# A small early store to the output, from a second DMA queue, in a pooling kernel that streams its input

**The chip and the metric.** One core of a Trainium2 chip. The metric is the device time of one execution in microseconds (us). A profile's span is some 1.8 us shorter than the device time of the same execution (92.5 for 94.24). Times in a trace are counted from the span's start. In this document "an engine" without a name is one of the core's 16 DMA engines. A transfer of 128 rows gives each engine 8 of them; in the trace's packet records a row is one packet. A transfer lands when the last engine has told that its rows are done.

## The reference

Average pooling over 2x2x2 windows of a float32 tensor. Cut to what matters:

```python
batch, channels, d, h, w = (8, 32, 32, 32, 32)      # kernel_size = 2
window = x[:, :, 2*i:2*i+2, 2*j:2*j+2, 2*k:2*k+2]
result[:, :, i, j, k] = np.mean(window, axis=(-3, -2, -1))
```

Seen as 256 rows (batch times channel), a row has 32,768 input elements (128 KB) and 4,096 output elements (16 KB). The input is 33.55 MB, the output 4.19 MB.

## The kernel before

The rows are taken in two halves of 128 partitions (t = 0, 1). Each half comes in by column blocks: six loads of 4 MB (rows of 32 KB), then four of 2 MB (rows of 16 KB). VectorE makes three passes over each block. Results collect in one tile for each half, which go out in three stores at the end.

```python
pool_in = ctx.enter_context(tc.tile_pool(name="pin", bufs=5))
pool_out = ctx.enter_context(tc.tile_pool(name="pout", bufs=1))
obuf = [pool_out.tile([P, 16 * KF], F32, name=f"obuf{t}") for t in range(2)]   # KF = 256
# ... cut: plan of loads; pool_unit = two tensor_adds and a tensor_tensor_reduce
for t, k0, parts in plan:
    tin = pool_in.tile([P, 32 * KF], F32, tag="tin", name="tin")
    for kb in parts:                       # shortened
        nc.sync.dma_start(out=v, in_=xv[t * P:(t + 1) * P, ...])
    # ... pool_unit on each part
for t, k0, kb in [(0, 0, 16), (1, 0, 14), (1, 14, 2)]:
    nc.sync.dma_start(
        out=ov[t * P:(t + 1) * P, k0 * KF:(k0 + kb) * KF],
        in_=obuf[t][:, k0 * KF:(k0 + kb) * KF])
```

All loads and stores are issued by the Sync engine (SP) and run in one DMA queue, in the order of issue: ten loads, then the stores of 2 MB, 1.79 MB and 256 KB.

Of the kernel before, what the change touches and what calls it, by code (L numbers as in the profile page):

```python
# [1 line left out]

# [4 lines left out]

F32 = mybir.dt.float32
KF = 256


@with_exitstack
def kernel(
    ctx: ExitStack,
    tc: tile.TileContext,
    x: bass.AP,
    kernel_size: int,
    out: bass.AP,
):
    nc = tc.nc  # L20
    assert kernel_size == 2, "only kernel_size == 2 supported"

    B, C, D, H, W = x.shape
    P = nc.NUM_PARTITIONS
    assert (B * C, D, H, W) == (2 * P, 32, 32, 32)
    add = mybir.AluOpType.add



    xv = x.rearrange("b c d h w -> (b c) (d h w)")  # L30
    ov = out.rearrange("b c d h w -> (b c) (d h w)")




    pool_in = ctx.enter_context(tc.tile_pool(name="pin", bufs=5))
    pool_out = ctx.enter_context(tc.tile_pool(name="pout", bufs=1))
    obuf = [pool_out.tile([P, 16 * KF], F32, name=f"obuf{t}") for t in range(2)]
    dummy = pool_out.tile([P, 1], F32, name="dummy")


    plan = [
        (0, 0, (32,)),
        (0, 32, (32,)),
        (0, 64, (32,)),
        (0, 96, (32,)),
        (1, 0, (32,)),
        (1, 32, (32,)),
        (1, 64, (16, 16)),
        (1, 96, (16, 16)),  # L50
    ]

    def pool_unit(buf, t, k0, kb):

        od = kb // 8
        a = buf.rearrange("p (o dd e) -> p o dd e", o=od, dd=2)
        b = buf[:, :od * 1024]
        nc.vector.tensor_add(  # L58
            out=b.rearrange("p (o e) -> p o e", o=od), in0=a[:, :, 0], in1=a[:, :, 1])
        bv = b.rearrange("p (e ww) -> p e ww", ww=2)  # L60
        c = buf[:, od * 1024:od * 1536]
        nc.vector.tensor_add(out=c, in0=bv[:, :, 0], in1=bv[:, :, 1])  # L62
        cv = c.rearrange("p (j hh k) -> p j hh k", hh=2, k=16)
        o0 = k0 * KF // 8
        nc.vector.tensor_tensor_reduce(  # L65
            out=obuf[t][:, o0:o0 + od * 256].rearrange("p (j k) -> p j k", k=16),
            in0=cv[:, :, 0], in1=cv[:, :, 1],
            scale=0.125, scalar=0.0, op0=add, op1=add, accum_out=dummy[:, :],
        )

    for t, k0, parts in plan:
        tin = pool_in.tile([P, 32 * KF], F32, tag="tin", name="tin")
        views = []
        o = 0
        for kb in parts:
            v = tin[:, o * KF:(o + kb) * KF]
            nc.sync.dma_start(
                out=v, in_=xv[t * P:(t + 1) * P, (k0 + o) * KF:(k0 + o + kb) * KF])
            views.append((v, k0 + o, kb))
            o += kb  # L80
        for v, k, kb in views:
            pool_unit(v, t, k, kb)
# [5 lines that stand above are left out]
            in_=obuf[t][:, k0 * KF:(k0 + kb) * KF],  # L88
        )


# [1 line left out]
_INS = ['x', 'kernel_size']  # L93
_OUTS = [((8, 32, 16, 16, 16), 'float32')]

_NUMBERS = {'kernel_size': 2}


# [26 lines left out]
```

## Time and profile before

| | before |
|---|---|
| device time, first three runs | 94.03 us (93.86 to 94.03) |
| span of the profiled run | 92.5 us |
| packets' time in the one DMA queue | 96.5% of 16 engines' span |
| VectorE busy | 64.0 us, 69% |
| end of VectorE's last pass | 85.95 us |

Read the DMA row first: a queue whose packets take 96.5% of the engines' span leaves the kernel little but to move fewer bytes or to move them in faster packets.

### The profile page before, as it was taken

To read this page: it belongs to the slowest core of one execution; us is meant where nothing else is said; L and a number is where in the kernel's file an instruction comes from. 1 tells how busy PE (TensorE), PEld (TensorE's weight loads), DVE (VectorE), ACT (ScalarE), POOL (GpSimd) and SP (SyncE) were. 2 spreads that over 40 slices of the span, in tenths; PEclk is the share of its full clock that TensorE was granted. 3 is DMA by queue.
4 is the path that set the end of the run, shared out by engine and by line. 5 is a ranking of instruction groups with operands and counts; after the bars stand their busy time and mean duration, and the time that the engine had idled before them with its cause. 6 is when DMAs were issued, how large, how long until landed. Compare 5 with 4: busy or idle time off the path is not lost.

```text
span 92.5 us, 103 instructions
## 1 busy us (share of the span) xinstructions
DVE 64.0 (69%) x40; POOL 0.2 (0%) x4
## 2 busy tenths in 40 slices
DVE  0000049992999299948996699849999999999100
POOL 0000000000000000000000000000000000000000
DMA  7699999998999999999989999989999999999992
GB/s 198 255 454 454 454 454 454 439 397 369 439 439 411 454 454 454 454 454 439 397 383 425 397 454 454 454 369 425 454 418 411 439 432 354 333 447 439 411 406 105
DMA packets 1872, 37.75 MB, mean 408 GB/s; under 512 B 208, under 2 KB 208, under 8 KB 336
## 3 DMA queue, kind: packets, MB, share of 16 engines
q1 hardware_dynamic: 1872, 37.75, 96.5%
HBM read 33.55 MB, written 4.19 MB: 408 GB/s over the span
## 4 chain that ended last, share of the span: by engine, by line
DMA 57%; DVE 35%; issue 0%; DVEq 0%
DMA tin<-in_x_dram 57%; DVE tin L58 19%; DVE tin L62 10%; DVE obuf L65 6%; DVE dummy L65 0%; DVEq L120 0%
## 5 line engine op out<-in xcount | busy, mean ns | idle before, releaser
L58 DVE TENSOR_TENSOR tin<-tin 128x4096 f32<-128x4096 f32 (+1 forms) x10 | 35.7, 3570 | 21.3 <-DMA tin<-in_x_dram 21.3
L62 DVE TENSOR_TENSOR tin<-tin 128x2048 f32<-128x2048 f32 (+1 forms) x10 | 18.6, 1865 | 0.3
L65 DVE CUSTOM_DVE_ANT_1 obuf<-tin 128x1024 f32<-128x1024 f32 (+1 forms) x10 | 10.1, 1011 | 0.3
L65 DVE DVE_READ_ACCUMULATOR2_ANT dummy<- 128x1 f32 x10 | 0.8, 82 | 0.0
L106 POOL MEMSET const-bfloat16-1.0<- 128x1 bf16 x1 | 0.1, 101 | 0.0
L106 POOL MEMSET const-uint8-127<- 128x1 uint8 x1 | 0.1, 101 | 0.0
L106 POOL MEMSET const-float32-0.0<- 128x1 f32 x1 | 0.1, 98 | 0.2 <-issue 0.2
L106 POOL MEMSET const-float32-1.0<- 128x1 f32 x1 | 0.1, 98 | 0.0
## 6 DMA issues: line engine op xcount, KB each, us to landing
tin<-in_x_dram SPq DMA_DIRECT2D x6, 4096.0 KB, 35.2
tin<-in_x_dram SPq DMA_DIRECT2D x4, 2048.0 KB, 38.0
out_dram<-obuf SPq DMA_DIRECT2D x1, 2048.0 KB, 36.6
out_dram<-obuf SPq DMA_DIRECT2D x1, 1792.0 KB, 9.1
out_dram<-obuf SPq DMA_DIRECT2D x1, 256.0 KB, 5.5
```

The lines of the kernel that those rows point to most:

```text
L58: nc.vector.tensor_add(out=b.rearrange("p (o e) -> p o e", o=od), in0=a[:, :, 0], in1=a[:, :, 1])
L62: nc.vector.tensor_add(out=c, in0=bv[:, :, 0], in1=bv[:, :, 1])
L65: nc.vector.tensor_tensor_reduce(out=obuf[t][:, o0:o0 + od * 256].rearrange("p (j k) -> p j k", k=16), in0=cv[:, :, 0], in1=cv[:, :, 1], s ...
L106: nc = _bacc.Bacc("TRN2", target_bir_lowering=False, num_devices=1)
```

## The change

Zeros are written early to the first 128 columns of the first 128 output rows. The likely intent is to have the first write to the output happen while the first load is only starting. The real store writes the same elements again later.

```diff
+    first = pool_out.tile([P, 128], F32, name="first")
+    nc.vector.memset(first[:, :], 0.0)
+    nc.scalar.dma_start(out=ov[0:P, 0:128], in_=first[:, :])
```

## The prediction

> **What bounds the kernel now.** The kernel reads 33.55 MB and writes 4.19 MB on one core, all from one DMA queue (the SP queue). I read the page first, then the two lists of waits (the engines' and the queue's own), then stretches of the span. The page's slices and its DMA part:
>
> ```profile
> DMA  7699999998999999999989999989999999999992
> GB/s 198 255 454 454 454 454 454 439 397 369 439 439 411 454 454 454 454 454 439 397 383 425 397 454 454 454 369 425 454 418 411 439 432 354 333 447 439 411 406 105
> q1 hardware_dynamic: 1872, 37.75, 96.5%
> HBM read 33.55 MB, written 4.19 MB: 408 GB/s over the span
> ```
>
> The DMA engines are busy from the first slice to the last but one; the packets' time is 96.5% of 16 engines' whole span of 92.5 us, that is 89.3 us of every engine. What is missing is 1.7 us in front and 1.4 us behind. A slice whose GB/s is low (the first two, and slices 34 and 35) is still full of busy engines: there packets are slow, not absent. Stretches cut at these places say it better (columns: stretch in us, its length, DVE busy, POOL busy, clock, DMA share, GB/s):
>
> ```profile
> 0.00:1.70 1.70, 0.00 (x0) 0.20 (x4) 1.00 0.00 0
> ...
> 4.10:50.00 45.90, 31.80 (x16) 0.00 (x0) 1.00 1.01 434
> 50.00:77.50 27.50, 23.92 (x17) 0.00 (x0) 1.00 0.98 419
> 77.50:80.00 2.50, 2.47 (x4) 0.00 (x0) 1.00 1.01 301
> 80.00:86.00 6.00, 5.85 (x7) 0.00 (x0) 1.00 1.01 432
> ```
>
> The sustained rate is 432 to 434 GB/s, 27 GB/s an engine. In the single packet records a 32 KB row takes 1.213 us, except the first one of each engine, which takes 1.39 to 2.09 us (mean 1.81): the start costs about 0.6 us an engine. At 77.5 to 80 us the rate falls to 301 GB/s: two 16 KB packets of each engine take about 1 us in place of 0.611. Over the 640 packets of that size the mean is 632.5 ns, so an engine, with 40 of them, loses 40 x 21.5 ns = 0.86 us, nearly all there.
>
> The chain on the page ends in VectorE work, and it is the wrong guide. The queue's own waits and the groups by form:
>
> ```profile
> SPq L86 <- DVE dummy L65: 44.0, 3, 31.3
> ...
> SPq L120 <- DMA out_dram<-obuf: 5.1, 1, 5.1
> ```
>
> ```profile
> L58 DVE TENSOR_TENSOR tin<-tin 128x2048 f32<-128x2048 f32 x4 | 9.1, 2286 | 0.0
> L62 DVE TENSOR_TENSOR tin<-tin 128x1024 f32<-128x1024 f32 x4 | 4.9, 1224 | 0.1
> L65 DVE CUSTOM_DVE_ANT_1 obuf<-tin 128x512 f32<-128x512 f32 x4 | 2.8, 692 | 0.1
> ```
>
> VectorE is through at 85.95 us; then the program waits 5.1 us for stores. The last store (256 KB) is issued at 85.98 us, but the 1.79 MB store in front of it, issued at 81.8 us, keeps the engines busy until 90.6 us. So VectorE is some 4.6 us early and the engines' queue sets the end: what adds time to an engine's packets adds it to the total, and what takes it away takes it from the total. The last 2 MB unit of VectorE (2.29 + 1.22 + 0.69 = 4.2 us) fits into that slack.
>
> **What the Trainium skill says.** "DMA: Bandwidth & Descriptors", section "Issuing engines are not separate DMA queues": DMAs of all issuers run on the same 16 engines and interleave; a second issuer saves only issue time. Nothing is to be saved here: the SP queue issues the first five loads from 0.73 to 3.14 us, and their data last until 51 us. That the second queue shares the engines, no trace of before shows, since it has one queue. The same page, "Queues, rings and completion order": an engine goes round its queues packet by packet. So the small store will not wait for the 20 MB of loads queued before it; it slips in between rows of the first load. Not visible before either. "Perfetto Trace Analysis", section "DMA Instruction — HWDGE (DVE, Sync)": the DMA instruction's span is only lock wait and descriptor generation, and the generator is used by one issuer at a time. The trace agrees as to the first: an issue takes 0.33 to 0.53 us, its data land 5.5 to 49 us later.
>
> **The change, part by part.** It removes nothing. It adds one tile of 128x128 zeros, a VectorE memset, one 64 KB store from the ScalarE queue, and a write-after-write order between that store and the real store of the same rows.
>
> *Memset.* VectorE adds 1024 elements a partition in 1.224 us and 2048 in 2.286: 1.04 ns an element and 0.16 us fixed. 128 elements are then about 0.3 us (my estimate), at about 0.7 us of the span, where VectorE is idle until 12.8 us. Cost on the path: 0.
>
> *Issue.* ScalarE can issue at about 1.0 us. The first load is issued at 0.73 and holds the descriptor generator until 1.11 us, so the store's descriptors come after it and the SP queue's second load, next at 1.16 us, may be held up by some 0.4 us. That load's first packet is needed only when the first load ends, at about 11.5 us. Cost: 0.
>
> *Data.* 128 rows of 512 B, 8 an engine. The size law from this trace: 84 ns for 2,048 B, 535 ns for 14,336 B, so 0.0367 ns a byte and 9 ns fixed; the 4 B semaphore writes, at 9 ns, agree. 512 B make 28 ns, eight 0.22 us, and with one semaphore write 0.23 us an engine. If all of it is added to a gapless engine the end moves 0.23 us. But it arrives at about 1.0 + 1.0 = 2 us (the first load took 1.0 us from issue to first packet), while each engine is in its slow first packet, which has about 0.6 us of waiting[...] in it. Writes from on-chip memory may be served in that hole. Cost: 0 to 0.23 us.
>
> *Order.* The real store must wait for the zeros. They land at 3 to 12 us, the real store is issued at 50.0 us and reached by the engines at about 81 us. One more semaphore check at most, a few tens of ns, behind 30 us of queued work. Cost: 0.
>
> *What it is meant to gain.* The slow stretch at 77.5 to 80 us comes while the first large store is next in line behind the last load: its first packets start at about 80.9 us, five to two packets after the slow ones. If the slowness is a first-touch cost of the output (taken ahead of the data, with the descriptors), the zeros pay it at the start instead, perhaps under the first load's own 0.6 us. That removes up to 0.86 us, and gives back what isn't hidden. Sum: between -0.86 and +0.23 us.
>
> **The rivals.**
>
> 1. *The slow stretch has nothing to do with the output*, and the store is plain extra traffic: 94.0 to 94.3 us. For it: no data are written to HBM before about 81 us, and the slow packets are over by 80 us; the second half of the input, first read at about 41 us, shows no such slowness (at most 0.06 us on a packet). I give this 0.65.
> 2. *The warm-up works*: 93.2 to 93.7 us. For it: it's the only slow stretch after the start, it stands just ahead of the first store, and all 16 engines have it at once. Against it: the points under 1, and that the cost may just move to the start, where it delays every load. I give this 0.22.
> 3. *The two queues disturb each other*: eight changes between reading HBM and writing it per engine, each emptying the pipeline. At up to 0.6 us each (the start-up loss) it would be as much as 4.8 us: 99 us. Against it: the one change of direction in the trace, load to store at about 81 us, costs nothing: packets stay at 0.611 us. A few tenths are more likely than several us. I give 0.1 to anything above 94.6 us, and 0.03 to over 2%.
> 4. *The late VectorE chain becomes the bound* because all loads land 0.23 us later. The last VectorE unit starts at 81.67 us and its load has landed by 81.64 us, so it would indeed slip, but 4.6 us of slack lie behind it. Time: as under 1.
>
> **Range and chances.** Weighing 94.15 (0.65), 93.4 (0.22) and 95 (0.1) gives about 94.07; I take 94.1. The 80% range is 93.4 to 94.6. Faster by 2% means under 92.15 us, and even the full removal of the slow stretch falls short of it; slower by 2% means over 95.9 us, which only rival 3 reaches.
>
> **What would show it.** A second queue with 128 packets and 0.07 MB, its packets within the first 3 to 12 us; the first load landing at 12.8 to 13.0 us; VectorE idle for the same 21 us or so; the end still a wait of about 5 us for stores. If the rate at 77 to 80 us stays near 300 GB/s, rival 1 holds; if it rises to 430, rival 2. I am wrong if the first load lands over 0.5 us later, if packets of the loads beside the zeros take much over 1.24 us, or if the SP queue waits for the zeros.

## The result

The changed kernel takes **94.05 us** (median of 6 fast runs, 93.81 to 94.22) against **94.03 us** (6 fast runs of the same rounds, 93.86 to 94.3). The ratio is 0.9997, with a 95% interval of 0.9976 to 1.0019. A ratio here is always the mean time of one kernel's fast runs over the mean of the other's of the same rounds, so it isn't quite the ratio of the medians.

The start of the changed kernel, from its timeline (start, duration, engine, line, what, count, idle time before):

```profile
0.73 2.40 SPq L82 DMA_DIRECT2D tin<-in_x_dram  x5
0.82 0.17 DVE L43 MEMSET first<- 128x128 f32 x1 [0.82 <-PEq L111]
1.02 0.42 ACTq L44 DMA_DIRECT2D out_dram<-first  x1
13.01 4.42 DVE L63 TENSOR_TENSOR tin<-tin 128x4096 f32<-128x4096 f32 x1 [12.02 <-DMA tin<-in_x_dram]
```

The first load is issued at 0.73 us as before. VectorE's first pass starts at 13.01 us, against 12.82 before: the first load lands 0.19 us later. The DMA part of the page:

```profile
DMA  7599999899999999998999999979999999999992
GB/s 227 241 443 461 461 450 440 369 411 397 440 454 454 454 454 454 440 454 354 411 397 440 454 454 454 454 340 447 425 418 418 447 447 383 340 411 454 423 396 96
q1 hardware_dynamic: 1872, 37.75, 96.3%
q10 hardware_dynamic: 144, 0.07, 0.2%
HBM read 33.55 MB, written 4.26 MB: 409 GB/s over the span
```

The second queue is there (q10): 128 rows and 16 semaphore writes, 0.2% of the engines' time. The low slices at the end are there too. Stretches of the changed kernel (stretch, length, DVE busy, POOL busy, clock, DMA share, GB/s):

```profile
5.80:14.50 8.70, 1.49 (x1) 0.00 (x0) 1.00 1.00 429
14.50:77.50 63.00, 54.04 (x31) 0.00 (x0) 1.00 1.01 432
77.50:80.00 2.50, 2.46 (x4) 0.00 (x0) 1.00 0.96 315
80.00:86.00 6.00, 5.89 (x6) 0.00 (x0) 1.00 1.00 429
```

and the same first stretch of the kernel before:

```profile
5.80:14.50 8.70, 1.68 (x1) 0.00 (x0) 1.00 1.00 433
```

From 5.8 to 14.5 us the engines are as full as before, with the packets of zeros among the loads'. The slow stretch at 77.5 to 80 us stays (315 GB/s; before 301). The end is a wait for stores as before, in the queue's own list of waits:

```profile
SPq L125 <- DMA out_dram<-obuf: 4.9, 2, 4.4
```

The landings in these two profiles, in us from the span's start:

| landing of | before | changed | difference |
|---|---|---|---|
| load 1 | 12.80 | 12.99 | +0.19 |
| load 2 | 22.51 | 22.71 | +0.20 |
| load 9 | 76.05 | 76.25 | +0.20 |
| load 10 (holds the slow stretch) | 81.63 | 81.69 | +0.06 |
| last store | 91.46 | 91.51 | +0.05 |

So in these two profiles the stream with the zeros is about 0.2 us later, and most of it comes back in the slow stretch. One pair of profiles doesn't show that the zeros did it: further profiles of the unchanged kernel, below, differ by more. That left three questions. Do the zeros really cost their traffic? What is the slow stretch? And is it shorter with the zeros, or was that chance?

The "excess" below is a number for the stretch, from the trace's packet records. The last four loads and the 2 MB store have 640 packets of 16 KB, 40 an engine, undisturbed 611 ns each. The excess is 40 times (their mean minus 611 ns). Before: 40 x (632.5 - 611) ns = 0.86 us an engine; changed: 40 x (627.5 - 611) ns = 0.66 us.

### The profile page after: what moved, and what is told of

The parts are those of the page before. It is cut to its first block, busy times and chain, and to the rows that moved or that the text cites. A ratio compares the mean times of both kernels' runs of the same rounds, so it can differ in the third digit from the quotient of the medians.

```text
span 92.4 us, 105 instructions
## 1 busy us (share of the span) xinstructions
DVE 64.2 (69%) x41; POOL 0.2 (0%) x4
## 4 chain that ended last, share of the span: by engine, by line
DMA 57%; DVE 35%; issue 0%; DVEq 0%
DMA tin<-in_x_dram 57%; DVE tin L63 19%; DVE tin L67 10%; DVE obuf L70 6%; DVE dummy L70 0%; DVEq L125 0%
```

## The experiments

Twelve runs were made, eight of new kernels and four of the two kernels again, all with the right result. The four that were only profiled have one execution each; from them only packets and landings are used. They used four chips; a ratio always compares two kernels on one chip.

### The changed kernel again

No edit.

> The changed kernel itself, again, with more rounds. Theory A (the zeros are plain extra traffic on engines without a gap): 0.2 us over before, ratio 1.002, first load landing 0.2 us later than before. Theory B (the extra traffic is paid back because the early write shortens the slow stretch at 77 to 80 us): ratio 1.000, and the slow stretch costs some 0.2 us an engine less than before in this profile too (in the first profile 40 x 16.0 ns = 0.64 us against 0.86). If the slow stretch here costs 0.8 us or more, the smaller one was chance.

Measured: 94.13 us against 94.14 us, ratio 0.9997 (0.9979 to 1.0016). Load 1 landed at 12.85 us, load 9 at 76.11 us, 0.05 us to 0.06 us later than in the first profile of before (12.80 and 76.05). The excess was 40 x (621.8 - 611) = 0.43 us. The time agrees with theory B, that something pays the traffic back. The interval ends at 1.0016, just short of theory A's 1.002.

### More zeros

```diff
-    first = pool_out.tile([P, 128], F32, name="first")
+    first = pool_out.tile([P, 1024], F32, name="first")
-    nc.scalar.dma_start(out=ov[0:P, 0:128], in_=first[:, :])
+    nc.scalar.dma_start(out=ov[0:P, 0:1024], in_=first[:, :])
```

> Eight times the bytes: rows of 4 KB, eight an engine, about 0.159 us each by the size law, 1.27 us an engine. Theory A: 95.3 us (1.3 over before), every load after the first landing 1.3 us later. Theory B or a hiding place at the start of about 0.6 us: 94.7 us or less.

Measured: 95.27 us, ratio 1.0115 (1.0093 to 1.0137), 1.13 us over before (94.14). In its trace a 4 KB row takes 159 ns, as worked out, and from load 2 (23.78 us, against 22.51 in the first profile of before) to load 9 (77.32, against 76.05) every landing is 1.27 to 1.28 us later: eight times 159 ns. That it fits to the hundredth is in part luck, since other profiles of before differ by up to 0.44 us at load 9. Hardly any of it hides at the start. At load 10 and the last store it is 1.17 us, as the slow stretch is again shorter (excess 0.64 us). Theory A holds up to the slow stretch.

For all of the first half's output the store is repeated four times:

```diff
+    for c in range(4):
+        nc.scalar.dma_start(
+            out=ov[0:P, c * 1024:(c + 1) * 1024], in_=first[:, :])
```

> Zeros over all of the first 128 output rows, in four stores of 512 KB: every byte that the first real store writes has been written before. Theory A: 32 x 0.159 = 5.1 us an engine, 99.1 us, slow stretch still there (rate near 300 GB/s for 2 us as the last load ends). First-touch theory: the slow stretch is gone, 98.2 us.

Measured: 98.72 us, ratio 1.0476 (1.0453 to 1.0499), 4.58 us over before. Every byte of the first real store has now been written before, and the slow stretch is still there, moved along with the last load. First the stretch at the old place, then at the new one:

```profile
77.50:80.00 2.50, 2.47 (x4) 0.00 (x0) 1.00 0.99 426
82.50:85.00 2.50, 2.47 (x4) 0.00 (x0) 1.00 1.04 367
```

The excess is 0.49 us. **So the slow stretch isn't the cost of a first touch of the output.** It came out shorter than in the first profile of before (367 GB/s against 301), but it did not go. Load 9 landed 4.97 us later than before, near the 32 x 0.159 = 5.1 us of traffic.

### The same queue

```diff
-    nc.scalar.dma_start(out=ov[0:P, 0:128], in_=first[:, :])
+    nc.sync.dma_start(out=ov[0:P, 0:128], in_=first[:, :])
```

> The same 64 KB of zeros, but issued on the SP queue ahead of the first load. The first load's issue must wait for the memset and one more issue: from 0.73 to about 1.45 us. Expected 94.6 to 94.9 us: 0.7 us of later start, with the 0.22 us of zero packets hidden in the first packets' slow start or not. A rival that says the queue makes no difference expects 94.05 us as the changed kernel.

Measured: 94.11 us, ratio 0.9995 (0.9975 to 1.0014). The expectation fell, because the kernel that was built isn't the one meant. Its timeline:

```profile
0.73 0.38 SPq L82 DMA_DIRECT2D tin<-in_x_dram  x1
0.82 0.17 DVE L43 MEMSET first<- 128x128 f32 x1 [0.82 <-PEq L111]
1.16 0.42 SPq L44 DMA_DIRECT2D out_dram<-first  x1
1.63 2.00 SPq L82 DMA_DIRECT2D tin<-in_x_dram  x4
```

The first load was put ahead of the store that waits for the memset, so it started on time. The zeros then ran in queue order, at 12.1 to 12.6 us, behind the first load's 128 rows. That load landed at 12.74 us, undelayed; load 9 landed 0.12 us late. The excess was 0.73 us. So the second queue isn't what keeps the price low: behind a load that is already issued, the one queue does as well, with 94.11 us for one queue and 94.13 us for two. This agrees with the Trainium skill, "DMA: Bandwidth & Descriptors", section "Issuing engines are not separate DMA queues". The store ahead of the first load, which was meant, stays untested.

### Where the slow stretch belongs

The first real store is moved to the ScalarE queue, in the kernel before, so that it starts when its data are ready, at 50 us:

```diff
-        nc.sync.dma_start(
+        (nc.scalar if t == 0 else nc.sync).dma_start(
```

> No zeros; the first real 2 MB store is issued on the ScalarE queue as soon as it is ready, at about 50 us, and so shares the engines with the loads. Question: what is the slow stretch at 77 to 80 us? If it belongs to the approach of the first large store, it moves to about 50 us and is absent at the end of the last load. If it belongs to the last load (its place in the queue or its addresses), it stays with the last load, which then lands some 5 us later. Time: the loads land up to 4.9 us later, so the last VectorE unit and the last store come late and a gap opens: about 95.5 us with the stretch, 94.7 without.

Measured: 95.96 us, ratio 1.0185 (1.0151 to 1.0218). The slow stretch moved. The store's first packet starts at 53.7 us in the trace's packet records. Around it, 33 of the loads' 32 KB packets, starting at 51.1 to 55.7 us, take 1.3 to 2.0 us in place of 1.213: 18 of them start up to 2.7 us ahead of the store's first packet on any engine, 15 up to 2.0 us after it (until 55.1 us only five packets of the store have started). Together they cost 0.78 us an engine, about what the stretch at the end had cost. All 16 KB packets take 611 ns: the excess is 0. The stretches just ahead of the store, at its start, and where the slow stretch stood before:

```profile
50.50:53.70 3.20, 2.04 (x1) 0.00 (x0) 1.00 0.88 328
53.70:56.50 2.80, 2.77 (x2) 0.00 (x0) 1.00 1.21 462
76.50:80.00 3.50, 3.47 (x4) 0.00 (x0) 1.00 1.00 431
```

The old place runs at 431 GB/s. The 328 and 462 are to be read with the DMA share beside them: the view counts a row where it starts, so in stretches this short the rate depends on the cut (from 50.5 to 54.2 us it is 403, from 54.2 to 57 us 339). Divided by the shares, 0.88 and 1.21, they are 373 and 382, both low. The packets' times are the evidence here. The time, 95.96 us, is over both times expected (95.5 and 94.7): a size missed, in a kernel whose loads land 4.9 us later.

In the second experiment the 2 MB store is issued after the 1.79 MB one, which needs VectorE's ninth unit. So nothing is queued behind the last load while it runs:

```diff
-    for t, k0, kb in [(0, 0, 16), (1, 0, 14), (1, 14, 2)]:
+    for t, k0, kb in [(1, 0, 14), (0, 0, 16), (1, 14, 2)]:
```

> No zeros; the 2 MB store is issued after the 1.79 MB one, so that nothing is queued behind the last load while it runs. If the slow stretch belongs to a store being next in line, it is absent from the last load, which lands at about 80.8 us in place of 81.6; the engines then idle for 1 to 2 us until the first store comes (issued at 81.8 us), 94.5 to 95.5 us in all. If it belongs to the last load itself, it stays at 77 to 80 us and the time is 95 to 96 us.

Measured: 95.94 us, ratio 1.0194 (1.017 to 1.0218). By time alone it would be the theory of the last load, whose range holds 95.94; the trace says otherwise:

```profile
77.50:80.00 2.50, 2.47 (x4) 0.00 (x0) 1.00 0.98 419
...
80.50:82.60 2.10, 2.06 (x4) 0.00 (x0) 1.00 0.00 0
82.60:86.00 3.40, 3.33 (x4) 0.00 (x0) 1.00 1.03 434
```

Now 77.5 to 80 us runs at 419 GB/s, the last load lands at 80.98 us, 0.65 us earlier than before, and no 16 KB packet takes longer than 640 ns. Then the engines stand still from 80.54 to 82.68 us: the store is issued at 81.83 us, when VectorE's ninth unit is done, and its packets start 0.84 us later. This idle time of 2.1 us is just over the 1 to 2 us expected, and it costs more than the shorter stretch brings.

**Both agree: the slow stretch belongs to the approach of the first large store.** It is in the loads' packets at the store's approach, in both places where the store stood, and it's absent when no store is queued there. Not every store brings it: in the run with 2 MB of zeros, the loads' rows after each engine's first, beside four stores of 512 KB, lost 0.13 us an engine in all. Is it the store's large rows? The 2 MB store in four pieces with rows of 4 KB, at the same place in the queue:

```diff
-    for t, k0, kb in [(0, 0, 16), (1, 0, 14), (1, 14, 2)]:
+    for t, k0, kb in [(0, 0, 4), (0, 4, 4), (0, 8, 4), (0, 12, 4), (1, 0, 14), (1, 14, 2)]:
```

> No zeros; the first real store cut into four of 512 KB with rows of 4 KB in place of 16 KB, at the same place in the queue. If the slow stretch comes from the large rows of the store that follows the last load, it shrinks or goes, worth up to 0.8 us: 93.4 us. If it comes from any large store following the loads, it stays and the 24 further packets of an engine cost 0.2 us at 9 ns: 94.3 us.

Measured: 94.02 us against 94.17 us, ratio 0.9987 (0.9968 to 1.0007): no difference that can be told from noise.

```profile
77.50:80.00 2.50, 2.47 (x2) 0.00 (x0) 1.00 1.00 315
```

The stretch stays, so rows of 16 KB in the store aren't needed for it. Nor is a store of 2 MB in one piece. What in a store's approach slows the packets ahead of it, no run shows.

### Is the stretch shorter with the zeros?

Two more profiles without the store of zeros, the first of the unchanged kernel, the second of the changed kernel with the store taken out. The first of them is the kernel before itself, with no edit:

> The kernel before, unchanged, for a second profile of its slow stretch. The first had 0.86 us an engine of excess over 611 ns a packet in the 16 KB packets; the three profiles with zeros on the second queue had 0.66, 0.43 and 0.58 us (over 611 ns). If the early zeros shorten the stretch, this shows 0.75 us or more. If the size of the stretch is chance, it may lie anywhere from 0.4 to 0.9.

```diff
-    nc.scalar.dma_start(out=ov[0:P, 0:128], in_=first[:, :])
```

> The changed kernel with the store of zeros taken out and the memset left in: no second queue, no early write. It should equal before in every landing (first load 12.8 us, ninth 76.05 us), 94.0 to 94.2 us. Its slow stretch is a third sample without early zeros: 0.75 us or more if zeros shorten it, anything from 0.4 to 0.9 if chance.

Then one that keeps the extra packets and takes away the early write, and one more profile of each kernel:

```diff
-    nc.vector.memset(first[:, :], 0.0)
-    nc.scalar.dma_start(out=ov[0:P, 0:128], in_=first[:, :])
+    nc.scalar.dma_start(out=first[:, :], in_=xv[0:P, 0:128])
```

> In place of the zeros, a load of the same shape (64 KB of the input into the small tile, never used), on the second queue at the start: the same extra packets, no early write to the output. Pure traffic: 0.16 to 0.23 us over before, ratio 1.002. If the early write is what shortens the slow stretch, the stretch here costs 0.75 us or more (over 611 ns a packet), as in two of the three profiles without zeros, and the end moves by the full 0.2 us. If the stretch's size is chance, the ratio is 1.000 to 1.002 all the same and the stretch anything from 0.4 to 0.9.

> The changed kernel, for a third profile of its slow stretch (0.66 and 0.43 us so far). Shortened by zeros: 0.7 or less. Chance: 0.4 to 0.9.

> The kernel before, for a third profile of its slow stretch (0.86 and 0.62 us so far; memset alone 0.90). Shortened by zeros in the other kernel: 0.75 or more here. Chance: 0.4 to 0.9.

Measured, all with the same last loads and stores:

| kernel | mean 16 KB packet, ns | excess, us an engine | load 9 lands, us |
|---|---|---|---|
| before, first profile | 632.5 | 0.86 | 76.05 |
| before, second | 626.4 | 0.62 | 76.49 |
| before, third | 632.6 | 0.86 | 76.23 |
| memset alone | 633.4 | 0.90 | 75.97 |
| changed, first profile | 627.5 | 0.66 | 76.25 |
| changed, second | 621.8 | 0.43 | 76.11 |
| changed, third | 626.4 | 0.62 | 76.46 |
| zeros in the same queue | 629.1 | 0.73 | 76.17 |
| small load in place of the zeros | 619.4 | 0.34 | 76.28 |

The small load took 93.96 us, ratio 0.9984 (0.9956 to 1.0011). The expectation of the second profile of before gives 0.58 us for a third profile with zeros on the second queue; by this formula the two with more zeros have 0.64 and 0.49 us. The memset alone (94.32 us), the second and third profiles of before (94.51 and 94.43 us) and the third of the changed kernel (94.34 us) have one profiled run each.

The means are 0.81 us in the four profiles without extra packets and 0.57 us in the three of the changed kernel. On the chip that ran three of these kernels the order is the same: 0.86 before, 0.62 changed, 0.34 with the small load. The timed runs point the same way: in all six sets with extra packets at the start the time rose by less than those packets take, for the four of 64 KB with ratios of 0.9984 to 0.9997 (intervals that end at 1.0011 to 1.0019) in place of 1.002. But 0.62 us stands on both sides and the zeros in the same queue have 0.73, so that the stretch is shorter with the zeros is likely and not shown. The excess also takes in single slow rows outside the stretch; from 76.5 us on alone it is 0.53 to 0.81 us without extra packets and 0.34 to 0.58 us in the changed kernel, which overlap as well. What can be said is that **a short stretch needs no early write**: the small load, which writes nothing to the output, has the shortest stretch of all, in its one profile. The idea that the early write is what shortens it fell there. The stretch's size isn't fixed either: one and the same kernel gave 0.62 and 0.86 us. Load 1 lands at 12.74 to 12.80 us in three of the four profiles without extra packets, and at 13.25 us in the fourth (before, second), so the start varies too, by more than the zeros cost.

## Why the prediction was right

The time was right (94.1 us predicted, 94.05 measured), and the bound as well. That it came within 0.05 us is luck: 94.1 is the mean of three outcomes (94.15, 93.4 and 95 us) weighted by their chances, and the zeros' own 0.2 us doesn't show in the timed runs. Point by point:

- **The bound.** That added packet time adds to the total is borne out at two sizes: 1.27 us of zeros made 1.13 us, 5.1 us made 4.58 us. In the profiles, part of the rest came back in the slow stretch (the last store lands 1.17 us and 4.70 us late). One reading is slightly off: the last row of the 1.79 MB store ends at 90.45 us, not 90.6.
- **Memset and issue cost nothing: right.** The memset took 0.165 us (0.3 estimated). The second load's issue stayed at 1.16 us; that it would be held up by 0.4 us was not seen, though the ScalarE issue at 1.02 to 1.44 us overlaps it. With the small load both issues start at 0.73 us and take 0.38 and 0.39 us, no longer than one alone (0.38). So that one issuer at a time uses the generator, as the prediction has it, doesn't show in these issues.
- **Data: the size was right, the place was wrong.** A row of 512 B took 27 ns (28 estimated), and the delay at load 2 was 0.20 us of the 0.23 worked out, in the first pair of profiles. The step that failed is that the zeros arrive "at about 2 us", in the hole of the first packets. In the three profiles of the changed kernel they start at 5.83, 5.99 and 6.00 us, after 48 rows of the load, three for each engine, and then take turns with it, one packet each. They land at 15.3 to 15.5 us, where the prediction had 3 to 12. So the hole of about 0.6 us wasn't used; what the engines wait for in their first packets, no run shows. The small load, issued in the same moment as the first load (0.73 us), started at 3.49 us, after one row for each engine.
- **Order: right.** The real store was issued at 50.20 us (50.01 before), later by what VectorE was later.
- **Rival 2, the warm-up: refuted.** With every byte of the first real store's target already written, the stretch remained (0.49 us, within the 0.43 to 0.66 us of the changed kernel).
- **Rival 1: right in its time, wrong in its reason.** The slow stretch does have to do with the output: it goes with the approach of the first large store. It's just not a cost of the first touch, and zeros don't remove it.
- **Rival 3, the queues' disturbance: not seen.** Even 32 changes an engine between reading and writing (2 MB of zeros) cost no more than their packets' time. In the changed kernel's first profile the loads' rows beside the zeros take 1.214 us on average.
- **Rival 4, VectorE as the bound: right.** Its last pass ends at 86.15 us, 0.2 us later than before, and the wait for stores behind it stays (4.9 us).

The 0.2 us of traffic doesn't show in the timed runs: two sets give 0.9997 each. It is no larger than the run to run differences (before: 93.86 to 94.3 us in six runs), and the slow stretch varies by more. How far the zeros themselves make the stretch shorter stays open.

## What to carry to other kernels

When the DMA engines are full from end to end, count packets and bytes: here an extra transfer at the start cost about 90% of its packets' time (1.13 of 1.27 us, 4.58 of 5.1 us), and one of 0.2 us was lost in other differences. A second queue bought nothing here, where the first queue's loads were issued in time. Test a warm-up idea by touching everything once, whatever that costs, and look whether the slow place in the profile is gone; the time alone would have hidden the answer here, twice. And take three profiles of one kernel before reading a cause into a few tenths of a microsecond.

## What the Trainium skill lacked or had wrong

- "DMA: Bandwidth & Descriptors", section "Queues, rings and completion order", has engines go round their queues packet by packet. The trace agrees once the zeros have started (one zero row, one load row). But a newly filled queue isn't served at the next packet: the zeros, issued at 1.02 us, came 4.8 to 5.0 us later, after three whole rows of 32 KB for each engine, in each of three profiles. The page lacks this.
- The same page, section "Latency and other measured facts", gives about 600 ns to the first byte for these queues and doesn't say from which moment. Here the first packet started 1.01 us after the start of its issue and 0.63 us after the end (0.73, 1.11 and 1.74 us); for a store on idle engines it was 0.84 and 0.49 us (81.83, 82.18 and 82.68 us). So the figure is near when it is counted from the issue's end. The first rows then took about 0.6 us longer than later ones (1.81 us on average, against 1.213), which it doesn't have.
- No page that was read has the slow stretch ahead of the first large store behind a stream of loads: 0.34 to 0.90 us an engine in thirteen profiles, absent in the one where no store was queued there.
